# The first load of a fused linear and LoRA kernel, split into four parts by partitions

## The chip, the cores and the metric

The kernel runs on one core of one Trainium2 chip. The metric is the device time of one execution in microseconds (us).

## The reference

```
y        = x_flat @ W                               # x: 32768 x 256, W: 256 x 256
lora_out = ((x_flat @ lora_A) * lora_E) @ lora_B    # rank 16
y        = y + scale * lora_out                     # float32 out, 32768 x 256
```

All inputs are float32, and scale is 1.0. x and the output are 33.5 MB each; W is 256 KB, lora_A and lora_B 16 KB each, lora_E 64 bytes.

## The kernel before

**Tiling.** The 32768 rows of x are 256 groups of 128. The kernel calls one group a "row" f, from 0 to 255: one row of x per partition, 1 KB each. The groups lie in six blocks (64, 32, 64, 24, 40, 32), and within a block each partition holds neighbouring rows of x, so that a load of n rows moves n KB of contiguous memory per partition. The buffer `ring` holds 184 such rows for each of the 128 partitions; loads write there, ScalarE writes the results over them in place, and stores read from there.

**The weights.** W + scale * lora_A diag(lora_E) lora_B is formed once: TensorE transposes lora_A (L272), VectorE multiplies by lora_E (L209), TensorE multiplies with lora_B (L276), and VectorE adds W (L220, `weff`). This set-up waits for three small inputs (`s_in` at 48: lora_A, lora_E and lora_B) and for W (`s_w`).

**The steps.** 32 steps of 8 rows follow. VectorE or GpSimd casts them to bf16 (`rounded`, L189), TensorE transposes them in pairs of bf16 read as float32 (L243), VectorE copies the result out of PSUM (L201), TensorE multiplies with `weff` (L259), and ScalarE copies the product back into the ring (L234).

**The order of the transfers** is written out by hand in `ORDER`: L8 is a load of 8 rows (1 MB), S64 a store of 64, W stands for the weights. SyncE issues all of it in that order; a load that reuses ring space waits for the store that frees it, and a store waits for TensorE's counter. Each load has a semaphore of its own, which gains 16 when a transfer has landed; the loads of the second round reuse the semaphores of the first.

**The start.** Two transfers are issued before the block `tc.tile_critical()` and its fence, so they go first: `early` holds the first load (8 rows, 1 MB, on SyncE's queue, L119) and lora_A (on ScalarE's queue, L123). Behind the fence SyncE issues W (L136), lora_E (L139), lora_B (L140), and then the loads. The other engines start their own work when SyncE has passed the fence.

Of the kernel before, what the change touches and what calls it, by code (L numbers as in the profile page):

```python
# [25 lines left out]
def kernel(  # L26
# [10 lines left out]
    nc = tc.nc  # L37
# [4 lines left out]
    x_flat = x.flatten_outer_dims()  # L42
# [4 lines left out]
    KC = K // P  # L47
# [7 lines left out]
    a_sb = const.tile([P, KC, R], FP32, name="a_sb")  # L55
    e_sb = const.tile([R, 1], FP32, name="e_sb")
    b_sb = const.tile([R, M], FP32, name="b_sb")
# [22 lines left out]
    loads = [(f, n) for kind, f, n in queue if kind == "L"]  # L80
# [6 lines left out]

    first = [f for f, _ in loads if f < RING]
    s_load = {f: sem(f"load_{f}") for f in first}
    landed = {f: 16 for f in first}  # L90
    for f, again in zip(first, [f for f, _ in loads if f >= RING]):
        s_load[again], landed[again] = s_load[f], 32

    s_last = sem("stores")
    s_store = {f: sem(f"store_{f}") for f, _ in stores if f < ROWS - RING}
# [1 line left out]
    s_in, s_w = sem("s_in"), sem("s_w")  # L97
# [6 lines left out]
    def rows_of(flat, f, n):  # L104
        first, rows = block_of[f]
        block = flat[first * P:(first + rows) * P, :].rearrange("(p b) k -> p b k", b=rows)
        return block[:, f - first:f - first + n, :]

    def place(f, n):
        return ring[:, f % RING:f % RING + n, :]  # L110
# [7 lines left out]
    def load(f, n):  # L118
        return nc.sync.dma_start(out=place(f, n), in_=rows_of(x_flat, f, n)).then_inc(s_load[f], 16)  # L119

    early = [
        load(*loads[0]),
        nc.scalar.dma_start(out=a_sb, in_=lora_A.rearrange("(p c) r -> p c r", c=KC)).then_inc(s_in, 16),  # L123
    ]
    for dma in early:
        tc.no_tile_sem_insts.add(dma.ins.name)
# [3 lines left out]

    with tc.tile_critical():  # L131

        freed = []
        for kind, f, n in queue[1:]:
            if kind == "W":
                nc.sync.dma_start(  # L136
                    out=w_sb, in_=W.rearrange("(p c) m -> p c m", c=KC)
                ).then_inc(s_w, 16)
                nc.sync.dma_start(out=e_sb, in_=lora_E[:, None]).then_inc(s_in, 16)  # L139
                nc.sync.dma_start(out=b_sb, in_=lora_B).then_inc(s_in, 16)  # L140
            elif kind == "L":
                for g, m in stores:
                    if g < f + n - RING and f - RING < g + m and g not in freed:
                        freed.append(g)
                        nc.sync.wait_ge(s_store[g], 16)
                load(f, n)
            elif kind == "S":

                half = (f + n) // H + 2
                if half <= ROWS // H:  # L150
                    nc.sync.wait_ge(s_m, half)
                else:
                    nc.sync.wait_ge(s_c, 1)
                nc.sync.dma_start(out=rows_of(out_flat, f, n), in_=place(f, n)).then_inc(
                    s_store.get(f, s_last), 16
                )

        for k in k_y:
# [4 lines left out]
            out=ident_f,  # L163
            in_=ident_f,
# [33 lines left out]
        def copied(n):  # L198
# [11 lines left out]
            out=ate,  # L210
# [119 lines left out]
```

## Time and profile before

| | |
|---|---|
| Time, median of three runs | 163.61 us (163.32 to 163.9) |
| The profiled execution | 163.32 us, its span 161.4 us |
| TensorE busy | 91.6 us (57% of the span) |
| VectorE, ScalarE, GpSimd busy | 60.0, 63.1, 33.0 us |
| DMA | 67.41 MB in 3521 packets, 418 GB/s over the span |
| SyncE's queue | 97.9% of 16 DMA engines' span |
| Mean granted TensorE clock | 0.82 |

The span runs from the first to the last instruction; the time of the execution has 1.9 us more around it. A line of the profile's slices cuts the span into 40 equal pieces of 4 us and gives the busy share of each in tenths. In the lists of instructions a name such as `SPq` means an engine's sequencer (here SyncE's) and "L119" a line of the kernel. For a transfer the listed time is that of issuing it, and not that of moving its bytes.

### The profile page before, as it was taken

Reading aid. Unit: us, or ns where it says so; the run is one execution under the profiler, and the core shown is the slowest. Engines: PE = TensorE matmul, PEld = TensorE weight load, DVE = VectorE, ACT = ScalarE, POOL = GpSimd, SP = SyncE. Lnnn points to the kernel's source line nnn. Section 1 sums busy time; section 2 is a strip of 40 time slices with the busy share of each in tenths; the row PEclk is TensorE's granted clock in tenths of the full one; section 3 lists DMA queues with packets and bytes.
Section 4 is the critical chain, followed back from the end, with each engine's and each line's share of the span. In section 5 each row is a group of like instructions: output and inputs, shape, how many; then the busy total and the mean of one; then the engine's idle time right before and its main releaser. Section 6 shows DMA issues by size and latency. Waiting matters only on the chain. (4 is left out here: it accounts for less than half of the span.)

```text
span 161.4 us, 1982 instructions
## 1 busy us (share of the span) xinstructions
PE 91.6 (57%) x780; PEld 82.2 (51%) x780; DVE 60.0 (37%) x52; ACT 63.1 (39%) x65; POOL 33.0 (20%) x21
## 2 busy tenths in 40 slices
PE   0189999999999950000079999999996000000000
PEld 0068899999799940000068999999994000000000
DVE  0196667783867400000076665866540000000000
ACT  3003676868576860000005868686777000000000
POOL 1004345422706200000062245314400000000000
PEclk9999999999999997555558999999999755555555
DMA  5999999999999998998999999999997989999993
GB/s 183 408 441 447 402 451 406 439 467 408 414 428 451 414 536 390 406 504 390 390 398 412 428 435 428 426 435 467 487 487 341 471 359 439 459 447 400 439 430 146
DMA packets 3521, 67.41 MB, mean 418 GB/s; under 512 B 560, under 2 KB 576, under 8 KB 704
## 3 DMA queue, kind: packets, MB, share of 16 engines
q1 hardware_dynamic: 3376, 67.39, 97.9%
q10 hardware_dynamic: 144, 0.02, 0.1%
q14 instruction: 1, 0.01, 0.0%
HBM read 33.85 MB, written 33.55 MB: 418 GB/s over the span
## 5 line engine op out<-in xcount | busy, mean ns | idle before, releaser
L234 ACT COPY ring<-py 128x1024 f32<-128x1024 f32 x64 | 61.8, 1015 | 60.1 <-PE py L259 60.1
L259 PE MATMUL py<-weff,xt 128*128 128x256 bf16 x512 | 63.3, 279 | 0.4 <-PEq L239 0.4
L259 PEld LDWEIGHTS py<-weff,xt 128*128 128x128 bf16 x512 | 51.1, 100 | 7.5 <-issue 1.0
L243 PE MATMUL pt<-ident_f,xb 128*128 128x128 f32 x264 | 36.8, 286 | 23.9 <-PEq L239 23.8
L189 POOL CAST xb<-ring 128x2048 bf16<-128x2048 f32 x15 | 32.3, 2151 | 81.2 <-PE pt L243 34.3
L201 DVE COPY xt<-pt 128x2048 bf16<-128x2048 bf16 x32 | 39.2, 1224 | 22.3 <-PE pt L243 22.0
L243 PEld LDWEIGHTS pt<-ident_f,xb 128*128 128x128 f32 x264 | 31.8, 148 | 25.3 <-issue 25.0
L189 DVE CAST xb<-ring 128x2048 bf16<-128x2048 f32 x17 | 20.7, 1221 | 30.7 <-DMA out_dram<-ring 24.9
L272 PE MATMUL py<-ident_f,a_sb 128*16 128x128 f32 x2 | 0.6, 394 | 7.0 <-DMA b_sb<-in_lora_B_dram 7.0
L272 PEld LDWEIGHTS py<-ident_f,a_sb 128*16 128x16 f32 x2 | 0.1, 88 | 7.0 <-issue 7.0
L207 DVE CAST b_bf<-b_sb 16x256 bf16<-16x256 f32 x1 | 0.3, 280 | 6.9 <-DMA b_sb<-in_lora_B_dram 6.9
L234 ACT ACT_TABLE_LOAD x1 | 1.3, 1283 | 1.4 <-SPq L131 1.4
L276 PE MATMUL py<-b_bf,ate 16*128 16x256 bf16 x2 | 0.6, 400 | 0.6 <-DVE ate L209 0.6
L276 PEld LDWEIGHTS py<-b_bf,ate 16*128 16x128 bf16 x2 | 0.1, 106 | 1.1 <-DVE ate L209 1.1
L220 DVE TENSOR_TENSOR weff<-w_sb,py 128x512 bf16<-128x512 f32 x1 | 0.7, 668 | 0.0
L209 DVE TENSOR_SCALAR ate<-py,e_sb 16x256 bf16<-16x256 f32 x1 | 0.5, 472 | 0.5 <-PE py L272 0.5
L160 POOL MEMSET ident_f<- 128x128 f32 x1 | 0.2, 205 | 1.2 <-SPq L131 1.2
L162 POOL TENSOR_SCALAR_AFFINE_SELECT ident_f<-ident_f 128x128 f32<-128x128 f32 x1 | 0.3, 294 | 0.2 <-POOL ident_f L160 0.2
L311 POOL MEMSET const-float32-0.0<- 128x1 f32 x1 | 0.1, 99 | 0.2 <-issue 0.2
L311 POOL MEMSET const-bfloat16-1.0<- 128x1 bf16 x1 | 0.1, 103 | 0.0
L311 POOL MEMSET const-uint8-127<- 128x1 uint8 x1 | 0.1, 102 | 0.0
L311 POOL MEMSET const-float32-1.0<- 128x1 f32 x1 | 0.1, 99 | 0.0
## 6 DMA issues: line engine op xcount, KB each, us to landing
ring<-in_x_dram SPq DMA_DIRECT2D x10, 2048.0 KB, 21.4
ring<-in_x_dram SPq DMA_DIRECT2D x3, 3072.0 KB, 41.8
out_dram<-ring SPq DMA_DIRECT2D x2, 4096.0 KB, 38.8
out_dram<-ring SPq DMA_DIRECT2D x1, 5120.0 KB, 35.1
ring<-in_x_dram SPq DMA_DIRECT2D x3, 1024.0 KB, 6.4
out_dram<-ring SPq DMA_DIRECT2D x1, 3072.0 KB, 36.1
w_sb<-in_W_dram SPq DMA_DIRECT2D x1, 256.0 KB, 5.1
out_dram<-ring SPq DMA_DIRECT2D x2, 40.0
```

The costliest lines, as they stand in the source:

```text
L162: nc.gpsimd.affine_select(out=ident_f, in_=ident_f, compare_op=mybir.AluOpType.not_equal, fill=1.0, base=0, pattern=[[-1, P]], channel_mul ...
L189: engine.tensor_copy(out=xbs[n % 2], in_=place(steps[n], G)).then_inc(k_x[n % 2], 1)
L201: nc.vector.tensor_copy(out=xts[n % 2].rearrange("p g r c -> p (g r c)"), in_=pts[n % 2].rearrange("p g r -> p (g r)").bitcast(BF16),).the ...
L207: nc.vector.tensor_copy(out=b_bf, in_=b_sb)
L209: nc.vector.tensor_scalar(out=ate, in0=ps_at, scalar1=e_sb, scalar2=float(scale), op0=mybir.AluOpType.mult, op1=mybir.AluOpType.mult,).the ...
L220: nc.vector.tensor_add(out=weff, in0=w_sb, in1=ps_aeb).then_inc(s_setup, 1)
L234: nc.scalar.copy(out=place(h * H, H), in_=pys[h % 2]).then_inc(k_y[h % 2], 1)
L243: return nc.tensor.transpose(pts[b][:, j, :], xbs[b][:, j, :].bitcast(FP32), ident_f)
L259: m = nc.tensor.matmul(pys[j // H][:, j % H, :], xts[b][:, j, :, c], weff[:, c, :], start=(c == 0), stop=(c == KC - 1),)
L272: t = nc.tensor.transpose(ps_at[:, c, :], a_sb[:, c, :], ident_f)
L276: m = nc.tensor.matmul(ps_aeb[:, c, :], ate[:, c, :], b_bf, start=True, stop=True)
L311: nc = _bacc.Bacc("TRN2", target_bir_lowering=False, num_devices=1)
```

## The change

The first load is cut into four transfers by partitions. With the step b and the start a, a part holds the partitions a, a + b, a + 2b and so on: (0, 8) has 16 partitions, (1, 2) has 64, (2, 4) has 32, and (4, 8) has 16, together 128. The first two are issued ahead of the fence, the other two are SyncE's first transfers behind it. All four count on the same semaphore, which therefore reaches 64 instead of 16, and 80 where the second round uses it again. On ScalarE's queue lora_E and lora_B take the place of lora_A ahead of the fence; lora_A goes on SyncE's queue, behind the parts of the first load and ahead of W. Everything after that stands in the same order as before on every engine.

```diff
-    landed = {f: 16 for f in first}
+    landed = {f: 64 if f == 0 else 16 for f in first}
     for f, again in zip(first, [f for f, _ in loads if f >= RING]):
-        s_load[again], landed[again] = s_load[f], 32
+        s_load[again], landed[again] = s_load[f], landed[f] + 16
...
+    def opening(*parts):
+        f, n = loads[0]
+        return [
+            nc.sync.dma_start(
+                out=place(f, n)[a::b], in_=rows_of(x_flat, f, n)[a::b]
+            ).then_inc(s_load[f], 16)
+            for a, b in parts
+        ]
+
     early = [
-        load(*loads[0]),
-        nc.scalar.dma_start(out=a_sb, in_=lora_A.rearrange("(p c) r -> p c r", c=KC)).then_inc(s_in, 16),
+        *opening((0, 8), (1, 2)),
+        nc.scalar.dma_start(out=e_sb, in_=lora_E[:, None]).then_inc(s_in, 16),
+        nc.scalar.dma_start(out=b_sb, in_=lora_B).then_inc(s_in, 16),
     ]
...
+        opening((2, 4), (4, 8))
         freed = []
         for kind, f, n in queue[1:]:
             if kind == "W":
                 nc.sync.dma_start(
+                    out=a_sb, in_=lora_A.rearrange("(p c) r -> p c r", c=KC)
+                ).then_inc(s_in, 16)
+                nc.sync.dma_start(
                     out=w_sb, in_=W.rearrange("(p c) m -> p c m", c=KC)
                 ).then_inc(s_w, 16)
-                nc.sync.dma_start(out=e_sb, in_=lora_E[:, None]).then_inc(s_in, 16)
-                nc.sync.dma_start(out=b_sb, in_=lora_B).then_inc(s_in, 16)
```

## Prediction

> **What bounds the kernel now.** I read the page's slices first, then its queue table, to see whether one resource is busy from end to end.
>
> ```profile
> PE   0189999999999950000079999999996000000000
> DMA  5999999999999998998999999999997989999993
> ...
> q1 hardware_dynamic: 3376, 67.39, 97.9%
> q10 hardware_dynamic: 144, 0.02, 0.1%
> ```
>
> The DMA row is full in every slice but the first (5) and the last (3), while TensorE rests in two long stretches. SyncE's queue (q1) keeps the 16 DMA engines 97.9% busy over the span and moves 67.39 MB; ScalarE's queue (q10) moves only lora_A. So the end is set by one stream of bytes. It can end earlier only by starting earlier or by losing its holes.
>
> Next came the waits of SyncE's own queue and its issues in time, to see whether anything that computes can hold the stream up.
>
> ```profile
> SPq L154 <- PE py L259: 64.6, 5, 29.2
> SPq L119 <- DMA out_dram<-ring: 38.6, 2, 31.8
> ...
> SPq L294 <- DMA out_dram<-ring: 35.0, 1, 35.0
> ```
>
> ```profile
> 0.74 0.39 SPq L119 DMA_DIRECT2D ring<-in_x_dram  x1
> 1.47 0.33 SPq L136 DMA_DIRECT2D w_sb<-in_W_dram  x1
> 1.86 0.42 SPq L139 DMA_DIRECT2D e_sb<-in_lora_E_dram  x1
> 2.33 0.41 SPq L140 DMA_DIRECT2D b_sb<-in_lora_B_dram  x1
> 2.78 5.02 SPq L119 DMA_DIRECT2D ring<-in_x_dram  x10
> 37.00 11.50 SPq L154 DMA_DIRECT2D out_dram<-ring  x2
> 80.31 10.02 SPq L119 DMA_DIRECT2D ring<-in_x_dram  x5
> ```
>
> SyncE waits long, but far ahead of the data: the first store is issued at 37.00, when loads that are queued already last to about 61 (the landing marks in the trace), and the last store, at about 124.6, is followed by 35.0 us in which SyncE only waits for transfers. TensorE's and VectorE's work may therefore move by many microseconds without moving the end.
>
> Last, the windows of the start (busy times, granted clock, DMA share, GB/s; bytes count at the start of their packet):
>
> ```profile
> 0.00:1.75 1.75, 0.00 (x0) 0.00 (x0) 0.00 (x0) 0.32 (x1) 0.32 (x5) 1.00 0.00 0
> 1.75:2.75 1.00, 0.00 (x0) 0.00 (x0) 0.00 (x0) 0.96 (x1) 0.38 (x2) 1.00 1.00 198
> 2.75:4.50 1.75, 0.00 (x0) 0.00 (x0) 0.00 (x0) 0.00 (x0) 0.00 (x0) 1.00 1.03 413
> 4.50:6.25 1.75, 0.00 (x0) 0.00 (x0) 0.00 (x0) 0.00 (x0) 0.00 (x0) 1.00 0.99 382
> ...
> 20.00:60.00 40.00, 38.28 (x348) 34.93 (x345) 24.14 (x21) 28.91 (x30) 14.43 (x7) 1.00 1.03 437
> ```
>
> Nothing moves until 1.75 us, which is 1.03 us after the first issue (the first packet starts at 1.77). Against the 437 GB/s of the long stretch the start then lacks 1.00 x (437 - 198) = 239 KB, 1.75 x (437 - 413) = 42 KB and 1.75 x (437 - 382) = 96 KB: together 377 KB, or 0.86 us. That is all a better start can win beyond the 1.75 us themselves.
>
> The trace's landing marks show where part of the 0.86 us sits. The 16 engines land their shares of the first load at 5.18 to 5.38 us for twelve of them, and at 5.59, 5.68, 5.80 and 5.83 for the other four. Each later load up to 53 us shows the same picture (twelve within 0.22, four later by 0.45 to 0.67). An engine that starts late stays late, and the last engine sets the end.
>
> **The change part by part.** The profiled execution took 163.32 us: a span of 161.4 and 1.9 around it. The median of the runs shown is 163.61, so 0.29 more; I add the sum to the median.
>
> *SyncE's issues.* Removed from its queue: e_sb and b_sb (0.42 and 0.41 us). Added: three more parts of the first load and a_sb. Consecutive issues are 0.39 to 0.47 us apart, and 0.73 us across the fence (0.74 to 1.47). So the parts issue at 0.74, 1.20, 1.93 and 2.39, a_sb at 2.85, W at 3.31, the second load at about 3.70 and not at 2.78: 0.92 us later. Data follows an issue by 1.03 us, so the second load could start at 4.73. Ahead of it lie 1.05 MB of x and 0.28 MB of weights, 1.33 MB or 3.05 us at 437 GB/s from 1.77 on: 4.82. The cover is 0.09 us at full rate and more at the rate that the start really has. Cost 0; if the cover goes, the delay counts one to one, up to 0.3 us if each issue takes 0.05 us more. Part two is there at 2.23, when part one's packets are still under way (almost no new packet starts from 2.00 to 2.50 in the profile: 49 GB/s). Parts three and four, there at 2.96 and 3.42, queue behind the 1.2 us of part two. Cost 0, at worst the 0.2 us of a second short hole.
>
> *Marks.* Three more transfers mean three more completion marks on each engine, 9 ns each in the packet records: +0.03 us.
>
> *a_sb behind the first load.* Its 128 packets of 128 bytes run between the packets of the first load today, eight per engine, and three engines show single 8 KB packets of 0.56 to 0.66 us right there (4.46 to 4.60 us) where 0.31 is normal. The change puts them behind the load, and only 16 packets each of e_sb and b_sb stay on ScalarE's queue. The four late engines can gain between 0 and the 0.45 us that separate them from the twelfth. I take the 0.45, since the stalls stand at those packets; that they cause them is inferred.
>
> *The small first part.* It has one packet per engine instead of eight. If the work before the first byte grows with the number of rows, the first bytes come earlier and the engines start closer together (today their first packets start from 1.77 to 2.33). The bounds are 0 and the first hole, 239 KB or 0.55 us. The nearest row speaks for the lower end: e_sb and b_sb with 16 rows took 0.42 and 0.41 us to issue, W with 128 rows 0.33. I take 0.15.
>
> [...] e_sb and b_sb, issued 0.47 us apart, landed at 6.4 and 6.9: 0.5 us apart. [...]
>
> *The set-up work.* PE L272 and DVE L207 wait for the last of the three small inputs until 6.9 to 7.0 us; then it is a_sb, behind x, at perhaps 6.0. The first products come up to 0.9 us earlier, W and the second load are late next. Worth 0: the stream covers it, as the waits show. ScalarE's second early issue and SyncE's (0.46 us) delay the release of ACT and POOL from 1.43 to about 1.9 us. POOL's identity matrix was ready at 2.4 and then is at 2.9, 3 us before its use. Worth 0.
>
> Sum: -0.45 - 0.15 + 0.03 = -0.57 us, span 160.8, 162.75 against the profiled 163.32, and 163.0 against the median.
>
> **The rivals.**
>
> *No change (163.5).* The late engines are late for another reason than a_sb, and a small part starts no sooner. For it: the issue times above don't grow with rows, and twelve engines are already together. The gain is then 0 to 0.4 us. It includes the case that the split does not do what it says, namely bring data earlier. [...]
>
> [...] If an engine's rate depends on which partitions are written together, parts of 16 rows in steps of 8 can run at half the rate. In the profile 1.05 MB takes 2.4 us at 437 GB/s. The two parts of 16 rows are 0.26 MB, 0.6 us: at half rate +0.6, hence 164.2. If the parts of 64 and 32 rows suffer too it is +2.4, hence 166.0. [...] Against it: b_sb, on 16 adjacent partitions, has packets of 46 ns for 1 KB, near the rate of the others, though too few to tell. [...]
>
> **How the numbers follow.** About 0.3% (0.5 us) is what a measurement of this kernel can tell from no change. The forecast (faster, 163.0) has 0.40: the start's deficit is real, is carried to the end and stands where the change acts. No change has 0.30. Slower has 0.30, of which 0.2 at about 164.2 and 0.1 above 164.8. The forecast's own range is 162.6 (both gains nearly whole: -1.0) to 163.1. The whole range reaches from 162.6 to 164.8, and leaves out the worst port case and a gain larger than the deficit.
>
> **What would show it.** In the windows of the changed kernel 1.75:2.75 should exceed 198 GB/s and 4.50:6.25 exceed 382; the landing marks of the second load should lie within about 0.3 us instead of 0.67 and end before 9.16. The no-change case shows the same four late engines. [...] The forecast is wrong if the second load lands as late as before, or if the end is set by other engines that are late for a reason after 53 us.

## The result and the profile after

The changed kernel is slower: a median of 166.06 us over five runs (164.81 to 166.39) against 163.45 for the kernel before (163.32 to 163.9), a ratio of 1.0131 (95% interval 1.0102 to 1.0161). The forecast was 163.0, with a range to 164.8. A second set of runs of the same kernel later gave 1.0137 (1.0111 to 1.0163). So the loss is 2.6 us between the medians and 2.1 to 2.2 us by the ratios; the text gives a loss by the medians where it does not say otherwise. The profiled execution took 166.39 us, its span 164.4 instead of 161.4. Two single executions of other kernels below, one of 207.82 us (of the split alone, and the only one of that kernel with a profile) and one of 540.67 us (of the first two loads made one), lie far outside and are left out of the ratios.

The page's slices and its queue table still show one stream without a pause, at a lower mean rate (410 GB/s against 418):

```profile
DMA  4999999999999998999899999999899899999990
GB/s 122 315 393 430 415 438 438 434 434 436 424 430 411 458 538 363 462 462 415 375 430 399 424 432 436 422 426 562 383 446 430 371 417 472 424 458 417 415 422 16
...
q1 hardware_dynamic: 3504, 67.39, 96.6%
```

The first three slices have 122, 315 and 393 GB/s where the page of before has 183, 408 and 441; from the fourth on the two agree within their scatter. SyncE's issues, and the spread of the four parts' issue times (ns, least, median and most), say why the start is late:

```profile
0.74 2.70 SPq L125 DMA_DIRECT2D ring<-in_x_dram  x4
3.48 0.58 SPq L148 DMA_DIRECT2D a_sb<-in_lora_A_dram  x1
4.10 0.43 SPq L151 DMA_DIRECT2D w_sb<-in_W_dram  x1
4.58 6.62 SPq L119 DMA_DIRECT2D ring<-in_x_dram  x10
40.75 11.50 SPq L167 DMA_DIRECT2D out_dram<-ring  x2
```

```profile
L125 SPq DMA_DIRECT2D ring<-in_x_dram x4: 480/576/597, 0.7 to 2.9; - x4
```

A part takes 0.58 us to issue (the median of the four), where the whole load took 0.39. W goes out at 4.10 instead of 1.47, and the second load at 4.58 instead of 2.78. The windows of the prediction, for the changed kernel:

```profile
0.00:1.75 1.75, 0.00 (x0) 0.00 (x0) 0.00 (x0) 0.00 (x0) 0.20 (x4) 1.00 0.00 0
1.75:2.75 1.00, 0.00 (x0) 0.00 (x0) 0.00 (x0) 0.48 (x1) 0.20 (x1) 1.00 0.50 143
2.75:4.50 1.75, 0.00 (x0) 0.00 (x0) 0.00 (x0) 0.80 (x1) 0.29 (x1) 1.00 0.96 293
4.50:6.25 1.75, 0.00 (x0) 0.00 (x0) 0.00 (x0) 0.00 (x0) 0.00 (x0) 1.00 0.91 307
6.25:20.00 13.75, 8.83 (x44) 6.52 (x44) 7.02 (x8) 1.69 (x2) 2.08 (x1) 1.00 1.01 398
20.00:60.00 40.00, 39.45 (x359) 36.09 (x358) 26.59 (x23) 28.43 (x31) 15.64 (x8) 1.00 1.01 433
```

Against before (198, 413, 382, then 435 from 6.25 to 20) the start lacks 55 + 210 + 131 KB and then 37 x 13.75 = 509 KB, together 905 KB, or 2.07 us at 437 GB/s. The engines rest mostly at first (a DMA share of 0.50 instead of 1.00 from 1.75 to 2.75). After that the share hardly falls (0.91 to 1.01), since the packets take longer (an 8 KB packet 0.43 us in the mean from 2.75 to 4.50 instead of 0.32, and 0.38 from 6.25 to 20 instead of 0.31): the engines count as busy at the lower rate.

A good part of the longer span is one engine. The mean of the last store's 16 landing marks is 1.66 us later than before (161.35 instead of 159.69), and so is the mean of the second load's (10.40 instead of 8.74), but the last mark of all is 3.06 us later. The landing marks of the second load lie at 9.65 to 11.32 us for fifteen engines and at 12.90 for the last (before: 8.50 to 9.16); those of the last store at 160.51 to 161.90 and 163.46 (before: 159.22 to 160.40). The last mark is 1.58 us behind the fifteenth at the second load, 1.56 at the last store, and between 1.53 and 1.60 at every load and store between them. The marks carry no engine's number; the steady gap says that it is one and the same engine, and that what it lost in the first microseconds it never made up. In the profiled execution of the second set, 164.83 us, no engine stands apart that far (second load 9.44 to 10.66, last store 160.15 to 161.90). Without its last engine the first execution would have ended its last store at 161.90 too. So the last engine accounts for the difference between these two executions; for the other runs, which have no profile, that is not shown.

Nothing changed where TensorE or VectorE work: SyncE's last wait for transfers is 34.4 us (35.0 before), and the first store is issued at 40.75 with more than 20 us of loads still queued.

### The profile page after: what moved, and what is told of

Read it like the earlier page. It is cut to its first block, busy times and chain, and to the rows that moved or that the text cites. A ratio compares the mean times of both kernels' runs of the same rounds, so it can differ in the third digit from the quotient of the medians.

```text
span 164.4 us, 1985 instructions
## 1 busy us (share of the span) xinstructions
PE 92.8 (56%) x780; PEld 82.8 (50%) x780; DVE 60.0 (37%) x52; ACT 63.2 (38%) x65; POOL 32.7 (20%) x21
## 5 line engine op out<-in xcount | busy, mean ns | idle before, releaser
L272 PE MATMUL py<-weff,xt 128*128 128x256 bf16 x512 | 64.2, 281 | 0.4 <-PEq L252 0.4
```

The costliest lines, as they stand in the source:

```text
L272: m = nc.tensor.matmul(pys[j // H][:, j % H, :], xts[b][:, j, :, c], weff[:, c, :], start=(c == 0), stop=(c == KC - 1),)
```

## The experiments

All ratios are to the kernel before, run beside each experiment. Theory A: the short parts leave the engines without queued work. Theory B: parts on some sets of partitions write slowly. Theory C: the small inputs cost. The edits are shortened. They stand against the change, but those of the fifth load and the one that joins the first two loads stand against the kernel before. The count that a load's semaphore reaches follows its number of parts.

| Kernel | Median us | Ratio (95% interval) |
|---|---|---|
| small inputs moved, first load whole | 163.42 | 0.9999 (0.9987 to 1.0011) |
| first load split, small inputs as before | 166.57 | 1.0188 (1.0169 to 1.0207) |
| four parts by rows | 164.99 | 1.0083 (1.0058 to 1.0107) |
| four parts of 32 partitions, step 4 | 165.94 | 1.0160 (1.0140 to 1.0179) |
| two parts of 64 partitions, step 2 | 163.81 | 1.0026 (1.0014 to 1.0039) |
| parts in the order 64, 32, 16, 16 | 165.69 | 1.0143 (1.0093 to 1.0193) |
| first load whole, issues behind it late | 163.54 | 1.0013 (1.0003 to 1.0022) |
| second load in four parts, step 4 | 163.65 | 1.0016 (1.0004 to 1.0027) |
| fifth load in parts, steps 8, 2, 4, 8 | 165.22 | 1.0117 (1.0095 to 1.0139) |
| fifth load in four parts, step 4 | 163.40 | 1.0005 (0.9994 to 1.0015) |
| fifth load in two halves, 0 to 63 and 64 to 127 | 168.59 | 1.0325 (1.0301 to 1.0350) |
| the change, second load ahead of lora_A and W | 165.06 | 1.0099 (1.0082 to 1.0116) |
| four parts, step 4, on two queues | 164.62 | 1.0077 (1.0053 to 1.0100) |
| first two loads made one | 163.37 | 1.0000 (0.9990 to 1.0010) |

**One half of the change at a time.** The first kernel keeps the load whole:

```diff
-        *opening((0, 8), (1, 2)),
+        *opening((0, 1)),
...
-        opening((2, 4), (4, 8))
```

> The first load stays whole; only lora_E, lora_B and lora_A change places as in the change. Theory A (each part of the split load finds its DMA engines empty, and the chain of issues on SyncE runs behind): 163.4 within 0.3 us, with the second load issued at about 2.6 us instead of 2.78. Theory B (parts on spaced partitions write slowly, whatever the queue holds): 163.4 too. Theory C (the new place of the small inputs is what costs): 165 or more.

Measured: 163.42, no difference. The second load was issued at 2.32. Theory C is out, and with it the gain that the prediction gave to moving lora_A. The first load itself did land earlier and closer together (its last mark at 5.51 instead of 5.83, 0.18 us behind the twelfth instead of 0.45), but the second load ended at 9.20 instead of 9.16: by then the gain was gone. The second kernel has the split and puts lora_A back on ScalarE's queue and lora_E and lora_B behind W:

```diff
         *opening((0, 8), (1, 2)),
-        nc.scalar.dma_start(out=e_sb, ...), nc.scalar.dma_start(out=b_sb, ...)
+        nc.scalar.dma_start(out=a_sb, ...)
...     # behind the parts: W, lora_E, lora_B
```

> The first load in the four parts of the change; lora_A, lora_E and lora_B stay where they were before. Theory A: 165 to 167 us, the second load issued near 5 us, three issues later than before. Theory B: 165 to 166.5 us, with slow packets in the first load alone. Theory C: 163.5.

Measured: 166.57, +3.1 us by the ratio, at the upper end for A. The whole loss is the split's. This kernel has one more issue ahead of the second load than the change (that load at 5.04 us in its profile), and its loss is larger; that the one follows from the other fits theory A and is not shown by itself.

**Parts in a place where the queue is full.** The fifth load (2 MB, landed at 23.8 us before) is issued at about 4.3 us and waits behind others. Three kernels cut it in different ways:

```diff
+        if f == 48:
+            for a, b in ((0, 8), (1, 2), (2, 4), (4, 8)):   # also: (0, 4), (1, 4), (2, 4), (3, 4)
+                nc.sync.dma_start(                          # also: [0:64] and [64:128]
+                    out=place(f, n)[a::b], in_=rows_of(x_flat, f, n)[a::b]
+                ).then_inc(s_load[f], 16)
+            return
```

> The kernel before, with the fifth load (2 MB, 16 rows) in the four parts by partitions (steps 8, 2, 4, 8) instead of the first one. It is issued where the queue holds several microseconds of work. Theory A: 163.5 within 0.4 us, since the parts wait behind other loads and no engine runs empty. Theory B: 164.7 us if only the two parts of 16 partitions run at half the rate (+1.2), up to 168.3 if all four do (+4.9).

> As the kernel before, with the fifth load (2 MB) in four parts of 32 partitions in steps of 4 (starts 0, 1, 2, 3), which is as many parts as in the run with steps 8, 2, 4, 8. [...] Rival D (any part costs a fixed time, whatever its partitions): 165.2, as with the steps 8, 2, 4, 8.

> The kernel before, with the fifth load (2 MB) in two parts by partitions, 0 to 63 and 64 to 127. [...] If the engines share by the count of partitions alone: 163.4.

Measured: +1.8, 0.0 and +5.2 us. The windows from 17.5 us on (last column GB/s), first before, then steps 8, 2, 4, 8, then step 4, then the halves:

```profile
17.50:25.00 7.50, 7.50 (x71) 7.00 (x69) 5.03 (x6) 5.79 (x6) 2.57 (x2) 1.00 0.99 419
25.00:30.00 5.00, 5.00 (x48) 4.66 (x47) 3.66 (x4) 3.66 (x4) 1.83 (x1) 1.00 0.99 423
```

```profile
17.50:25.00 7.50, 7.28 (x68) 6.56 (x66) 4.14 (x4) 5.24 (x6) 2.88 (x1) 1.00 1.00 326
25.00:30.00 5.00, 4.52 (x40) 3.75 (x39) 3.58 (x3) 2.79 (x4) 2.88 (x1) 1.00 0.99 416
```

```profile
17.50:25.00 7.50, 7.50 (x72) 7.00 (x70) 4.99 (x6) 5.79 (x6) 2.58 (x2) 1.00 1.00 424
25.00:30.00 5.00, 5.00 (x48) 4.67 (x46) 3.66 (x5) 3.68 (x4) 1.82 (x1) 1.00 1.03 439
```

```profile
17.50:25.00 7.50, 7.50 (x70) 6.83 (x68) 4.20 (x4) 5.71 (x6) 2.86 (x1) 1.00 1.08 238
25.00:30.00 5.00, 1.60 (x15) 1.19 (x13) 0.63 (x1) 2.00 (x3) 0.53 (x1) 0.90 0.90 272
```

The halves run at 238 GB/s, 0.57 of the 419 beside it, and lose 181 x 7.5 + 151 x 5 = 2.11 MB, 4.8 us, on a load that takes 4.9 us whole. Their 16 KB packets mostly take 1.2 us instead of 0.61: half rate. With steps 8, 2, 4, 8 the loss is 93 x 7.5 + 7 x 5 = 0.73 MB, 1.7 us. The packet records place it: 16 KB packets take 0.61 us in the parts of 64 and 32 partitions, and mostly 0.7 to 1.2 us in the two parts of 16 and in about two packets of each engine behind them. Four parts in steps of 4 lose nothing, so it is not the number of parts. Theory B holds: 64 neighbouring partitions run at about half rate (238 GB/s where the load before has 419), and so do 16 partitions 8 apart (packets of mostly 0.7 to 1.2 us instead of 0.61); 64 in steps of 2 (0.61 us) and 32 in steps of 4 (0.61 us, and 424 GB/s with all four parts in such steps) run at the full one. The runs show these rates and not their reason.

**The same at the start.** If B made the loss, parts in steps of 4, or cut by rows, would be free there too.

```diff
-        *opening((0, 8), (1, 2)),       ...       opening((2, 4), (4, 8))
+        *opening((0, 4), (1, 4)),       ...       opening((2, 4), (3, 4))
```

> As the change, but the first load is cut into four parts of 32 partitions in steps of 4, two ahead of the fence and two behind. Theory A + B: the part of the loss that comes from half-rate parts (about 0.9 us: two parts of 16 partitions at half the packet size of the fifth load, which lost 1.8) is gone, and what the late issues cost is left: 164.3 to 165.2 us. Theory B alone: 163.4. Theory A alone: as the change, 164.8 to 166.4.

```diff
-                out=place(f, n)[a::b], in_=rows_of(x_flat, f, n)[a::b]
+                out=place(f + r, 2), in_=rows_of(x_flat, f + r, 2)      # r = 0, 2 | 4, 6
```

> As the change, but the four parts are cut by rows: each part is 2 rows of all 128 partitions (256 KB, packets of 2 KB), so every part writes all partitions. Theory A: 164.8 to 166.4 us, as the change, since the issues are as many and as late. Theory B: 163.3 to 163.9, since no part is on few partitions.

Measured: 165.94 and 164.99. Without any slow set of partitions the start loses 2.6 us, at least as much as in the change; cut by rows it loses 1.4 us by the ratio and 1.6 by the medians. The expectation of A + B, that 0.9 us would come back with step 4, was wrong. A reading of it, not shown by itself, is that half rate costs nothing more where the engines wait anyway. The finer windows, before, then the change, then step 4:

```profile
2.75:3.75 1.00, 0.00 (x0) 0.00 (x0) 0.00 (x0) 0.00 (x0) 0.00 (x0) 1.00 1.05 433
3.75:5.00 1.25, 0.00 (x0) 0.00 (x0) 0.00 (x0) 0.00 (x0) 0.00 (x0) 1.00 0.92 350
5.00:6.25 1.25, 0.00 (x0) 0.00 (x0) 0.00 (x0) 0.00 (x0) 0.00 (x0) 1.00 1.07 417
...
7.50:10.00 2.50, 1.31 (x6) 0.74 (x6) 2.33 (x4) 0.00 (x0) 0.00 (x0) 1.00 1.12 475
```

```profile
2.75:3.75 1.00, 0.00 (x0) 0.00 (x0) 0.00 (x0) 0.80 (x1) 0.29 (x1) 1.00 0.90 194
...
5.00:6.25 1.25, 0.00 (x0) 0.00 (x0) 0.00 (x0) 0.00 (x0) 0.00 (x0) 1.00 0.90 273
```

```profile
2.75:3.75 1.00, 0.00 (x0) 0.00 (x0) 0.00 (x0) 0.75 (x1) 0.29 (x1) 1.00 0.99 385
3.75:5.00 1.25, 0.00 (x0) 0.00 (x0) 0.00 (x0) 0.00 (x0) 0.00 (x0) 1.00 0.95 275
5.00:6.25 1.25, 0.00 (x0) 0.00 (x0) 0.00 (x0) 0.00 (x0) 0.00 (x0) 1.00 0.62 201
...
7.50:10.00 2.50, 1.31 (x6) 0.73 (x6) 2.20 (x3) 0.00 (x0) 0.00 (x0) 1.00 1.01 365
```

With step 4 the engines are only 0.62 busy from 5.00 to 6.25 us: lora_A and W, issued at 3.42 and 4.05, arrive when the parts are used up. From 3.75 to 5.00 they count as busy at 275 GB/s: there the third part, issued behind the fence, comes when the first two are nearly used up, and its first packets take up to 1.09 us, the packets behind them 0.31. In the change the same falls on the second part, since the first has one packet per engine: from 2.75 to 3.75 there are 194 GB/s, and twelve 8 KB packets take over 0.6 us, up to 1.09.

**Two parts, and another order.**

```diff
+        *opening((0, 2), (1, 2)),          # no part behind the fence
```

> As the change, but the first load is cut into two parts of 64 partitions in steps of 2, both ahead of the fence; each part is four packets, 1.24 us, per engine. Theory A: 163.4 to 163.9, since a part of 1.24 us covers the 0.6 us until the next issue. Theory B: 163.4. Rival D (every part costs): about +0.5 us, 163.9.

```diff
+        *opening((1, 2), (2, 4)),       ...       opening((0, 8), (4, 8))
```

> The change with its parts in the order 64, 32, 16, 16 partitions instead of 16, 64, 32, 16: the 64 and the 32 go ahead of the fence. Theory A: a first part of 1.24 us per engine covers the next issue, so the hole after it goes; the later parts are as short as in the change. 163.8 to 165.0, less than the change. Theory B alone: as the change minus nothing, 164.8 to 166.4.

Measured: 163.81 and 165.69. Two parts cost 0.45 us; the first packet comes 0.3 us later, at 2.08 us instead of 1.77, as with every first part by partitions, and that may be most of it. Of the order 64, 32, 16, 16 theory A expected at most 165.0; that was a miss, for the loss is as large as the change's. The window from 2.75 to 3.75 is better than in the change (280 GB/s instead of 194) and the one from 5.00 to 6.25 worse (206 instead of 273): the hole comes later, around the last parts.

**Is it the late queue, or the short part?** The first load whole, with three tiny transfers where the parts were, so that lora_A, W and the second load (3.71 us) go out as late as with the parts by rows (3.73):

```diff
-        *opening((0, 8), (1, 2)),
+        *opening((0, 1)),
+        nc.sync.dma_start(out=spare[0], in_=lora_E[:, None]).then_inc(s_spare, 16),
...
-        opening((2, 4), (4, 8))
+        for i in (1, 2):
+            nc.sync.dma_start(out=spare[i], in_=lora_E[:, None]).then_inc(s_spare, 16)
```

> The first load whole, the small inputs placed as in the change, and three tiny transfers (lora_E into spare tiles) on SyncE's queue where the change has its parts two to four; lora_A, W and the second load are issued as late as with the parts cut by rows (second load near 3.7 us). Theory A in the form 'the holes between short parts': 163.4 to 163.7, since the first load is one piece and covers the issues. Theory A in the form 'the queue behind runs late': 164.5 to 165.

Measured: 163.54, +0.2. At the same lateness the parts by rows lose 1.4 us by the ratio. A whole load of 2.4 us covers that chain of issues; four pieces of it do not. Now the reverse, the first load whole and the second in four parts:

```diff
+        if f == 8:
+            for a, b in ((0, 4), (1, 4), (2, 4), (3, 4)):
...
```

> The first load whole, the small inputs placed as in the change, and the second load (1 MB) cut into four parts of 32 partitions in steps of 4. It has the same short parts and nearly the same moment as the first load cut that way (165.94), but 1 MB, lora_A and W stand in the queue ahead of it. Theory A (a short part costs only where nothing stands ahead of it to cover the next issue): 163.4 to 163.9. Rival E (short parts cost anywhere in the first 10 us, since these engines are slow then): 165 or more.

Measured: 163.65, +0.3, where the same parts cost 2.6 one place earlier. Rival E is out: what counts is whether work is queued ahead of the part. Of the second load's 128 packets only two take over 0.6 us here; of the first load's, cut the same way, 22 do.

**How much is the chain of issues?** The first kernel issues the second load ahead of lora_A and W; the second shares the four parts between two queues:

```diff
-    "L8", "W", "L8", "L16",
+    "L8", "L8", "W", "L16",
```

> The change with the second load issued ahead of lora_A and W, right behind the four parts, so about 1.1 us earlier (near 3.5 us instead of 4.58). Theory A1 (the chain of issues on SyncE is longer than the data that it carries; the engines wait for the second load): 0.5 to 1 us of the loss comes back, 164.5 to 165.2. Theory A2 (each short part starts its engines cold, whatever follows): as the change, 165.5 to 166.1.

```diff
-        *opening((0, 8), (1, 2)),       ...       opening((2, 4), (4, 8))
+        *opening((0, 4), (1, 4), (2, 4), (3, 4)),     # odd starts on ScalarE's queue
...
+        nc.scalar.dma_start(out=e_sb, ...)            # behind the fence
+        nc.scalar.dma_start(out=b_sb, ...)
```

> The first load in four parts of 32 partitions, two on SyncE's queue and two on ScalarE's, all ahead of the fence; lora_E and lora_B follow on ScalarE's queue, lora_A, W and the second load on SyncE's, the latter near 3.2 us. Theory A1: close to the first load in two parts (163.8), up to 164.2. Theory A2: as the four parts on one queue, 165.6 to 166.3.

SyncE's issues in the first kernel, and then in the second:

```profile
0.74 2.70 SPq L125 DMA_DIRECT2D ring<-in_x_dram  x4
3.48 0.58 SPq L119 DMA_DIRECT2D ring<-in_x_dram  x1
```

```profile
0.74 1.18 SPq L125 DMA_DIRECT2D ring<-in_x_dram  x2
2.27 0.36 SPq L147 DMA_DIRECT2D a_sb<-in_lora_A_dram  x1
2.69 0.42 SPq L150 DMA_DIRECT2D w_sb<-in_W_dram  x1
3.15 7.70 SPq L119 DMA_DIRECT2D ring<-in_x_dram  x10
```

The issues moved as meant: the second load at 3.48 in the first kernel, at 3.15 in the second. Measured: 165.06, some 0.5 us better than the change (1.0099 against 1.0131 and 1.0137, intervals that overlap, so that this gain is not clear of noise), and 164.62, 1.3 us better than the same parts on one queue (ratios 1.0077 and 1.0160, clear of noise). By these the chain of issues would be a quarter to a half of the loss (A1); the second kernel also changes the queue of two parts, so the half is not shown to be the chain's alone. The 1.2 us that are left in the second kernel lie above the 163.8 to 164.2 that A1 expected. The load in two parts sent its second load at 3.15 us as well and lost 0.45 us (1.0026 against 1.0077, clear of noise): short parts cost something even when issued early (A2).

**The same kernel again, and the opposite.**

> The changed kernel once more, beside these: its five runs lay in two groups, 164.8 to 164.9 and 166.1 to 166.4. Theory A has no reason for a gap; a chance stall of one engine, as in the profiled run, would show again as a group near 166 and another near 164.9, with the landing marks of one engine apart from the rest in the first alone.

Measured: 165.51 (164.83 to 165.86), without a gap between groups. The lag of the last engine differs between the two profiled executions, 1.58 us and 0.2 at the second load. In the first profile a single 8 KB packet of the second load took 2.5 us; what held that engine up stays open.

```diff
-    "L8", "W", "L8", "L16", "L16",
+    "L16", "W", "L16", "L16",
```

> The kernel before, with the first two loads (8 rows each) made one of 16 rows: the opposite of the change, more data per issue at the start. Theory A: the same as before or up to 0.3 us faster (163.1 to 163.4), since the start of before already has its issues covered. If the first step's later data mattered, it would be slower by up to 2.4 us.

Measured: 163.37, no difference. The start of the kernel before is already covered; no version here beats it beyond the noise.

## Why the prediction was wrong

- **The bound** was right: one stream of transfers sets the end, a delay of the start comes out at the end (the mean landing mark is 1.66 us later at the second load, some 1.9 from the third to the tenth, and 1.66 at the last store), and TensorE's work (first store at 40.75 instead of 37.00) costs nothing.
- **"SyncE's issues" is the step that failed, and both of its zeros.** The first is the delay of the second load, "Cost 0". It took 0.39 to 0.47 us from issue to issue and 0.73 across the fence, prices of transfers over all 128 partitions or of small ones. The parts stand 0.53 to 0.66 us apart and 0.93 across the fence, lora_A behind the last part took 0.58 too, and the first part's bytes start 1.38 us after its issue (2.12) and not 1.03. The second load went out at 4.58 instead of 3.70, 0.88 us later, against a cover that the step itself put at 0.09. It named the price (one to one) and bounded the delay at 0.3 us; the rows of before held no part by a step of partitions, and a bound from them should have been wider. The cover itself was reckoned well for a whole first load: with the second load sent at 3.71 behind it only 0.2 us were lost.
- **"At worst the 0.2 us of a second short hole"** is the second zero, and the larger miss. With the second load out at 3.48 us, earlier than the 3.70 that the step reckoned with, the change still loses 1.6 us by the ratio, and four parts on two queues, with the second load at 3.15, lose 1.2 by the medians. The window from 2.75 to 3.75 fell from 433 to 194 GB/s, 239 KB or 0.55 us, although part two was issued before part one's bytes came: part one's packets had ended by 2.9 us, and the first packets of part two took up to 1.09 us instead of 0.31, much as the first packets of all did in the kernel before (up to 1.04). How the rest of the loss divides between such cold starts, with nothing queued ahead, and the late queue stays open, and so does why such a first packet is slow.
- **The two gains** (0.45 and 0.15 us) did not come. With lora_A moved and the load whole the first load did end earlier, by 0.32 us, and its four late engines were gone, but the second load ended as late as before. So the step that failed there is the one that carried a gain of the first load to the end; what took it back before the second load, and whether lora_A's packets had made the engines late, is not settled. The small first part brought the first bytes later (2.12 us instead of 1.77).
- **The slower rival** named 164.2 up to 166, which all but holds the number (166.06, later 165.51), but by the wrong mechanism, so that it fits by luck. The half rate in its sum was the author's estimate, which no row of before shows. The fifth load does show about half (238 GB/s in halves where the load before has 419), but at the start four parts in steps of 4, which kept the full rate at the fifth load (424 GB/s), lose 2.6 us, as much as the change. A rate below 413 GB/s from 2.75 to 4.50 us, as the slower rival would have it (293 measured), stands with step 4 at the start too (385 from 2.75 to 3.75, 275 from there to 5.00) and so can't tell the two apart.
- **The range** ended at 164.8, because the only slow case priced was a half rate of some parts. No run shows the write ports by which the range names that case; what the runs show is a rate that depends on which partitions a part holds (0.57 of the full one for the halves of the fifth load). An uncovered chain of issues and one cold start, 0.88 + 0.55 us, would have given 164.9 from 163.45, still below the 165.5 to 166.1 that were measured.

## What to carry to other kernels

In a stream that is full from end to end, what is lost at the start comes out at the end (here 1.66 us in the mean landing mark of the second load and 1.66 in that of the last store), so the first transfer has to be long enough to cover all issues up to the next long one: add up the issue times, and compare with the bytes in flight (a whole load of 2.4 us covered a second load issued at 3.71 us but for 0.2 us). Price an issue by a row of the same shape, and if there is none, bound it by twice the nearest, which is an estimate from these runs (0.58 us for a part where the nearest row had 0.39); the issue right behind it can take as long (0.58 us for lora_A). When a load must be cut, cut it where the queue is full and so that each part spreads over the partitions as the whole does (here steps of 4 cost nothing at the fifth load and a part in steps of 2 had packets of 0.61 us, while neighbours cost 5.2 us and steps 8, 2, 4, 8 together 1.8).

## What the runs showed of the hardware

- On SyncE's queue a transfer over 16, 32 or 64 partitions picked by a step took 0.47 to 0.64 us to issue, one over all partitions mostly 0.33 to 0.45. One over all partitions that was issued right behind such a part took 0.58 as well (lora_A in the change, the second load where it was put ahead of lora_A and W). As the first transfer of the queue a part by partitions had its first packet 0.3 us later (2.07 to 2.12 us instead of 1.74 to 1.77).
- Four parts of 32 partitions in steps of 4 cost 2.6 us as the first load, 0.3 as the second and nothing as the fifth (which has 2 MB instead of 1).
- Lags between the 16 DMA engines last: 1.58 us between the last two landing marks at 12.90 us were 1.56 us at 163.46, and never under 1.53 between.
